# Giving the tiles of a decoder layer their own starting bytes in SBUF

## The chip, the core and the metric

The kernel runs on one core of a Trainium2 chip. The metric is the device time of one execution in microseconds; the runs of the kernel before took 2301.84 and 2302.49 us, median 2302.16 us. In the tables, PE is TensorE's matmul, PEld its weight load (the stationary operand), DVE, ACT and POOL are VectorE, ScalarE and GpSimd, and SP is the engine that issues nearly all transfers.

## The reference, cut to what matters

One decoder layer over 1024 positions of width 1024, in float32: a half feed-forward layer (SwiGLU, hidden width 2816), a mixer of two attentions with 8 heads of 64 each, a second half feed-forward layer, and a gated embedding.

```
x = x + 0.5 * swiglu(rms_norm(x, ffn1_norm), w_gate, w_up, w_down)
h = rms_norm(x, mix_norm)
fq, fk, fv, f_logit, sq, sk, sv, g_fox, g_sb = split_columns(h @ w_in)
y_fox = forgetting_attention(rms_norm(fq), rms_norm(fk), fv, log_f)
y_sb  = stick_breaking_attention(sq, sk, sv)
merged = sigmoid(g_fox) * (y_fox @ w_branch_fox) + sigmoid(g_sb) * (y_sb @ w_branch_sb)
x = x + merged @ w_out
x = x + 0.5 * swiglu(rms_norm(x, ffn2_norm), ...)
x = x + sigmoid(rms_norm(x, ple_norm) @ w_ple_gate) * (p @ w_ple_proj)
```

## The kernel before, in words

Each large product is written as float32 operands split in two: a rounded high part (fp32r) and the low remainder. A product is then three passes of matmuls, high by high, high by low, low by high, each with a stationary operand of 128 x 128 and a moving operand of up to 128 x 512. The two feed-forward layers and the output projection save matmuls by seven products of quarter blocks for eight, with sums of blocks formed beside.

The stages, by the profile's time: the start (0 to 41 us), the gate and up products of the first feed-forward layer (line 469, 41 to 473), its down product (line 364, 473 to 680), the projections of the mixer and the attention (lines 696, 704, 854, 935, 936, 987, 1009, 680 to 1417), the two branch products (line 1210, 1417 to 1478), the output projection (line 364), the second feed-forward layer (lines 424 and 469 to 1990, line 364 to 2197), and the gated embedding (line 1477, to the end). The order of the work on every engine is written out by hand.

Nearly all SBUF data passes through one pool, `sb`. The helper `slot(tag, shape)` takes the next buffer of a tag; the tags and their numbers of buffers stand in `BUFS`, and the buffers of a tag are used in turn. What the tags hold where the matmuls read them:

- line 469 (`product`): stationary is `hl`, a split weight block that rotates through the tags WL, WL, WL, Q, Q, PT; moving is one of seven blocks of activations `B[m]`: `B[1]`, `B[2]`, `B[5]`, `B[6]` in H, `B["12"]`, `B[7]` and `B[4]` in X, and `B[3]` in four T.
- line 364 (`matmuls` in `make_down`): both operands are in H, taken one after the other in `prep`, the activations (stationary) first and the weights (moving) second.
- lines 704 and 1210: stationary WH or WL (and others of a few), moving H. Lines 696 and 1477: stationary H, moving WH, WL, T, GF, RN, PT, Y. In the first eight units of line 696 the moving block has rows of 264 columns, 1056 bytes, so its four pieces begin 0, 32, 64 and 96 bytes further on modulo 256.
- line 1009: stationary X (the values), moving PT. Lines 935 and 936: stationary Q, moving KH and KL.

During a matmul PE also loads the stationary operand of the next one; the two operands of which this text speaks are those: the moving operand of one matmul, and the stationary operand that is loaded beside it. By "offset" is meant the first byte of the one less that of the other, modulo 256.

Where the buffers begin follows from the sizes and the order in which the pool meets the tags. In the kernel before, the first bytes modulo 256 are:

| tag | X | PT | H | T | WH | KH, KL | WL | Y | Q | GF, RN, RAW |
|---|---|---|---|---|---|---|---|---|---|---|
| buffers 1, 2, ... | 128, 128 | 128 x3 | 128 x4 | 128 x4 | 128, 0, 128 | 0, 0 | 0, 128, 0 | 128, 0 | 128, 128 | 128, 128 |

WH, WL and Y differ among themselves because their largest tile has 4224 bytes and not 4096.

Of the kernel before, what the change touches and what calls it, by code (L numbers as in the profile page):

```python
# [18 lines left out]
P = 128  # L19
# [10 lines left out]
PSUM = {"sc": 3, "pt": 2, "av": 1, "pf": 2}  # L30
BUFS = {"X": 2, "H": 4, "RAW": 2, "WH": 3, "WL": 3, "T": 4, "GF": 2, "RN": 2,
        "Q": 2, "KH": 2, "KL": 2, "Y": 2, "PT": 3}
FQ, FK, FV, FL, SQ, SK, SV, GFOX, GSB = 0, 512, 1024, 1536, 1544, 2056, 2568, 3080, 4104


@with_exitstack
def tile_hybrid_decoder_layer(
# [6 lines left out]
    nc = tc.nc  # L44
    cp = ctx.enter_context(tc.tile_pool(name="const", bufs=1))
    st = ctx.enter_context(tc.tile_pool(name="stats", bufs=4))
    sb = ctx.enter_context(tc.tile_pool(name="sb", bufs=2))
# [4 lines left out]
    def nm(s):  # L52
        uid[0] += 1
        return f"{s}_{uid[0]}"

    def slot(tag, shape, dt=F32):
        return sb.tile(shape, dt, tag=tag, bufs=BUFS[tag], name=nm(tag))

    def stat(shape, tag, bufs=4):
        return st.tile(shape, F32, tag=tag, bufs=bufs, name=nm(tag))  # L60
# [51 lines left out]
    def wraw_load(pieces, nk, n, tag="RAW"):  # L112
        raw = slot(tag, [P, nk, n])
        c = 0
        for src in pieces:
            w = src.shape[-1]
            nc.sync.dma_start(raw[:, :, c:c + w], src)
            c += w
        return raw
# [5 lines left out]
    def whigh(raw, nk, n, tag):  # L125
        hi = slot(tag, [P, nk, n], F32R)
        order("wh", nc.scalar.copy(hi[:], raw[:]))  # L127
        return hi

    def wlow(raw, hi, nk, n, tag, eng_lo=nc.gpsimd):  # L130
        lo = slot(tag, [P, nk, n], F32R)
        if nk == 1:
            parts = [(slice(None), slice(None), slice(i * n // 2, (i + 1) * n // 2)) for i in range(2)]
        else:
            parts = [(slice(None), slice(i * nk // 2, (i + 1) * nk // 2)) for i in range(2)]
        for part in parts:
            ins = eng_lo.tensor_sub(lo[part], raw[part], f(hi[part]))  # L137
            if eng_lo is nc.gpsimd:
                order("wl", ins)
        return lo  # L140
# [900 lines left out]
    def mix_start():  # L1041

        mx["v"], mx["qk"] = {}, {}
        mx["u1"] = v_units(FV + 256, NH, mx["v"])
        tags = (("T", "GF"), ("T", "Y"))
        mx["u2"] = fox_qk_units(FOX_PAIRS[0], mx["qk"], tags, "KH")
        q0 = FOX_PAIRS[0] * P
        pieces = [[kp(win)[:, 4 * kh:4 * kh + 4, a:a + n] for a, n in cols] for cols in (((FV + 256, 256 + NH),), ((FQ + q0, P), (FK + q0, P))) for kh in range(2)]
        raws = {}

        def load_v(X):
            raws["v"] = [wraw_load(pieces[kh], 4, 256 + NH, "Y") for kh in range(2)]

        def split_v(X):
            mx["v"]["w"] = [wsplit(raws["v"][kh], 4, 256 + NH, NAT[kh]) for kh in range(2)]

        def load_qk(X):
            raws["qk"] = [wraw_load(pieces[2 + kh], 4, 256) for kh in range(2)]

        def end(X, N):  # L1060
            hT.extend(halves(N))
            store_x(X, 1)
            for cell in loads[:2]:
                cell[1] = None
            side = posts(N[1], (24, 64, 104, 144), lambda: bank("pt"))
            side[48] = [lambda: mx["qk"].update(w=[wsplit(raws["qk"][kh], 4, 256, tags[kh]) for kh in range(2)])]
            weave(seq(*[g for _, g in mx["u1"][:4] + mx["u2"][:4]]), side)
        return {3: [load_v], 4: [split_v], 5: [lambda X: store_x(X, 0)], 6: [load_qk], "end": end}
# [164 lines left out]
    X = [slot("X", [P, 4, D]) for _ in range(2)]  # L1233
# [86 lines left out]
    X, N = ffn(N, ffn1_w_gate, ffn1_w_up, ffn1_w_down, mix_norm[0], x[0], ad[0], tags, first_entry, mix_start())  # L1320
# [178 lines left out]
    X, hT = [], []  # L1499
# [34 lines left out]
```

## Time and profile before

| | |
|---|---|
| median of two runs | 2302.16 us |
| profiled execution: span | 2300.6 us |
| instructions in it | 30661 |
| granted TensorE clock | 0.999 |
| PE busy, PEld busy | 2269.6, 1913.6 us |
| DVE, ACT, POOL busy | 1468.0, 980.7, 829.9 us |

The span runs from the first to the last instruction of the profiled execution; the runs' time holds some 1.6 us more. A row of the groups names the line, the engine, the operation, what is written and read (`ps<-H,WL`: the moving operand H, the stationary WL), the shape, the count, the busy time and the mean in ns of one. The duration of a matmul in these rows reaches from its start to the modelled end of its pipeline and so is longer than the distance to the next start: 12 matmuls with a mean of 389 ns begin 227 ns apart. A difference of durations between two groups of the same shape is nevertheless a difference of that distance, since the rest of it is the same.

### The profile page before, as it was taken

The page shows a single profiled execution, that of the slowest core. Times are in us where ns is not written, and L with a number is a line of the kernel's source. Part 1 is how long each engine was busy: PE and PEld are TensorE (multiplying, and loading weights), DVE is VectorE, ACT ScalarE, POOL GpSimd, SP SyncE. Part 2 cuts the span into 40 slices and gives each one's busy share as a digit, 9 for nine tenths or more (in the row PEclk, how much of TensorE's full clock was granted, in tenths as well). Part 3 has the DMA queues.
Part 4 walks back from the last instruction along what each step waited for, and adds up shares of the span by engine and source line. Part 5 has one row for each costly group of instructions (what it writes and reads, how often), then busy time and mean ns, then how long its engine had stood idle before and what let it go on. Part 6 is the DMA issues. An engine that isn't in the chain of part 4 may idle for free.

```text
span 2300.6 us, 30661 instructions
## 1 busy us (share of the span) xinstructions
PE 2269.6 (99%) x11466; PEld 1913.6 (83%) x11466; DVE 1468.0 (64%) x2199; ACT 980.7 (43%) x1742; POOL 829.9 (36%) x762
## 2 busy tenths in 40 slices
PE   9999999999999999899999999999999999999999
PEld 6888888888888999798988778888888888888887
DVE  8855555588863566456656766789645454778753
ACT  6433333333442555555555554246333333334431
POOL 2344444300033556545455645400534343200111
PEclk9999999999999999999999999999999999999999
DMA  3232323484332122422133235732423232655232
GB/s 138 92 124 83 124 83 123 142 307 168 103 120 75 52 79 74 137 79 71 50 82 89 74 115 199 258 139 74 138 78 128 78 128 78 226 213 205 70 106 92
DMA packets 188279, 275.49 MB, mean 120 GB/s; under 512 B 27097, under 2 KB 110297, under 8 KB 188130
## 3 DMA queue, kind: packets, MB, share of 16 engines
q1 hardware_dynamic: 188128, 273.53, 35.4%
q8 instruction: 90, 1.47, 0.3%
q14 instruction: 59, 0.48, 0.1%
q10 hardware_dynamic: 2, 0.00, 0.0%
HBM read 189.83 MB, written 75.27 MB: 115 GB/s over the span
## 4 chain that ended last, share of the span: by engine, by line
PE 55%; DVE 2%; ACT 1%; issue 0%; DVEq 0%; ACTq 0%
PE ps L469 18%; PE ps L364 12%; PE ps L704 9%; PE ps L1477 4%; PE ps L1210 4%; PE ps L1009 2%; PE ps L696 2%; PE ps L987 2%; DVE RN L911 1%; PE ps L424 1%; PE ps L936 1%; PE ps L935 1%; PE ps L854 1%; PE ps L224 0%; DVE H L104 0%
## 5 line engine op out<-in xcount | busy, mean ns | idle before, releaser
L364 PE MATMUL ps<-H,H 128*128 128x512 f32 x2184 | 497.8, 389 | 1.2 <-DVE X L372 1.2
L364 PEld LDWEIGHTS ps<-H,H 128*128 128x128 f32 x2184 | 409.3, 188 | 86.8 <-issue 2.0
L469 PE MATMUL ps<-H,WL 128*128 128x512 f32 x1008 | 244.6, 394 | 0.6 <-ACT WL L103 0.6
L469 PEld LDWEIGHTS ps<-H,WL 128*128 128x128 f32 x1008 | 189.7, 188 | 44.7 <-ACT WL L103 1.0
L704 PE MATMUL ps<-H,WH 128*128 128x512 f32 x768 | 209.5, 401 | 2.1 <-DVE PT L819 2.1
L137 POOL TENSOR_TENSOR WL<-RAW,WH 128x512 fp32r<-128x512 f32 (+1 forms) x108 | 129.4, 1219 | 101.2 <-ACT WH L127 72.9
L704 PEld LDWEIGHTS ps<-H,WH 128*128 128x128 f32 x768 | 136.8, 188 | 26.3 <-DVE PT L819 3.0
L990 DVE TENSOR_TENSOR PT<-ps,PT 128x512 fp32r<-128x512 f32 (+1 forms) x160 | 101.2, 633 | 84.4 <-ACT PT L989 83.6
L137 POOL TENSOR_TENSOR WL<-Y,WH 128x512 fp32r<-128x512 f32 (+1 forms) x10 | 14.4, 1465 | 383.1 <-ACT WH L127 383.1
L469 PE MATMUL ps<-H,Q 128*128 128x512 f32 x600 | 143.9, 390 | 0.0
L372 DVE SCALAR_TENSOR_TENSOR X<-ps,X 128x512 f32<-128x512 f32 x168 | 109.0, 685 | 50.9 <-PE ps L364 50.9
L696 PE MATMUL ps<-WH,H 128*128 128x256 f32 (+1 forms) x896 | 131.7, 286 | 2.0 <-ACT RN L753 0.7
L469 PEld LDWEIGHTS ps<-H,Q 128*128 128x128 f32 x600 | 112.6, 188 | 24.5
L989 ACT CAST PT<-ps 128x512 fp32r<-128x512 f32 (+1 forms) x160 | 87.2, 547 | 106.7 <-PE ps L987 102.1
L469 PE MATMUL ps<-X,WL 128*128 128x512 f32 x504 | 123.8, 394 | 0.0
L696 PEld LDWEIGHTS ps<-WH,H 128*128 128x128 f32 x896 | 116.5, 189 | 4.1 <-ACT RN L753 0.9
L469 PEld LDWEIGHTS ps<-X,WL 128*128 128x128 f32 x504 | 94.9, 188 | 22.0
L1009 PE MATMUL ps<-PT,X 128*128 128x256 f32 (+1 forms) x640 | 104.4, 283 | 8.8 <-DVE PT L990 8.8
L1009 PEld LDWEIGHTS ps<-PT,X 128*128 128x128 f32 x640 | 94.7, 190 | 21.0 <-DVE PT L990 11.0
L704 PE MATMUL ps<-H,WL 128*128 128x512 f32 x384 | 108.6, 404 | 0.0
L948 POOL TENSOR_TENSOR T<-T,l 128x128 f32<-128x128 f32 (+3 forms) x64 | 73.3, 1149 | 89.6 <-DVE l L947 87.2
L911 DVE TENSOR_TENSOR_SCAN RN<-GF,RN 128x127 f32<-128x127 f32 (+2 forms) x96 | 102.2, 1065 | 2.7
(400 smaller groups left out, 4680.0 us busy)
## 6 DMA issues: line engine op xcount, KB each, us to landing
hidden<-PT SPq DMA_DIRECT2D x40, 512.0 KB, 3.1
WH<-in_ffn_w_gate_dram SPq DMA_DIRECT2D x38, 512.0 KB, 5.0
Q<-hidden SPq DMA_DIRECT2D x24, 512.0 KB, 6.4
hidden<-RN SPq DMA_DIRECT2D x22, 512.0 KB, 2.6
RAW<-in_w_in_dram SPq DMA_DIRECT2D x22, 512.0 KB, 4.1
KH<-in_ffn_w_up_dram SPq DMA_DIRECT2D x20, 512.0 KB, 5.8
KL<-in_ffn_w_up_dram SPq DMA_DIRECT2D x20, 512.0 KB, 6.6
T<-in_ffn_w_down_dram SPq DMA_DIRECT2D x20, 512.0 KB, 4.4
```

What stands on the lines that cost most here:

```text
L137: ins = eng_lo.tensor_sub(lo[part], raw[part], f(hi[part]))
L364: pe(nc.tensor.matmul(groups[g][t][:], act[:, a, k, t * P:(t + 1) * P], wt[:, b, k, :], start=(fresh and n == 0), stop=(i in (6, 1, 4) and ...
L372: nc.vector.scalar_tensor_tensor(xs, groups[g][t][:], scale, xs, ALU.mult, ALU.add)
L469: pe(nc.tensor.matmul(ps[:], hl[:, a, k, :], rhs(m, b, k), start=(first and i == 0), stop=(final and i == 11), skip_group_check=True))
L696: pe(nc.tensor.matmul(ps[:, :n], hT[t // 4][a][:, k, (t % 4) * P:(t % 4 + 1) * P], w[k // 4][b][:, k % 4, :n], start=(i == 0), stop=(i == ...
L704: pe(nc.tensor.matmul(ps[:], w[a][:, k, :], hT[half][b][:, k, :], start=(i == 0), stop=(i == 23)))
L911: order("dve", nc.vector.tensor_tensor_scan(*args))
L989: high = nc.scalar.copy(pt[:, 0, :width], ps[:, :width])
L990: low = nc.vector.tensor_sub(pt[:, 1, :width], ps[:, :width], f(pt[:, 0, :width]))
L1009: pe(nc.tensor.matmul(o, lh, r, start=(kpair == c and i == 0), stop=(kpair == 0 and i == 3)))
L1210: pe(nc.tensor.matmul(ps[:], w[a][:, k, :], yT[g][b][:, k, half * 512:half * 512 + 512], start=(i == 0), stop=(i == 11)))
L1477: pe(nc.tensor.matmul(ps, hT[t // 4][a][:, k, (t % 4) * P:(t % 4 + 1) * P], pl["w"][d, k // 2][b][:, k % 2, cs], start=(i == 0), stop=(i = ...
```

## The change

Three things are changed, and all are about where in SBUF the tiles lie.

`slot` no longer takes a buffer of the size that is asked for, but one of a fixed size for each tag (`SIZE`, in elements of four bytes), and hands out a piece of it that begins `PLACE[tag]` elements into it. All the sizes are multiples of 256 bytes, so that all buffers begin at the same byte modulo 256, which is 128 in the built program. On that phase, the places put the tiles as follows (bytes beyond it, buffer by buffer):

| tag | X | H | WL | Q | PT | all others |
|---|---|---|---|---|---|---|
| bytes | 0, 96 | 0, 64, 0, 32 | 0, 64, 16 | 32, 96 | 0, 192, 8 | 0 |

The larger buffers need room, and the scratch that is kept for transfers whose descriptors are made on GpSimd is cut from 16384 to 8192 bytes a partition.

```
+SIZE = {"X": 4096 + 64, "H": 4096 + 64, "RAW": 1088, "WH": 1088, "WL": 1088 + 64, "T": 1024, "GF": 1024, "RN": 1024,
+        "Q": 1024 + 64, "KH": 1024, "KL": 1024, "Y": 1088, "PT": 1024 + 64}
+PLACE = {"X": (0, 24), "H": (0, 16, 0, 8), "WL": (0, 16, 4), "Q": (8, 24), "PT": (0, 48, 2)}
...
+    turns_of = {}
+
     def slot(tag, shape, dt=F32):
-        return sb.tile(shape, dt, tag=tag, bufs=BUFS[tag], name=nm(tag))
+        n = 1
+        for d in shape[1:]:
+            n *= d
+        i = turns_of.get(tag, 0)
+        turns_of[tag] = i + 1
+        o = PLACE.get(tag, (0,))
+        o = o[i % BUFS[tag] % len(o)]
+        t = sb.tile([P, SIZE[tag]], dt, tag=tag, bufs=BUFS[tag], name=nm(tag))[0:shape[0], o:o + n]
+        if len(shape) == 2:
+            return t
+        names = "abcd"[:len(shape) - 1]
+        return t.rearrange(f"p ({' '.join(names)}) -> p {' '.join(names)}", **dict(zip(names, shape[1:])))
...
-    nc = _bacc.Bacc("TRN2", target_bir_lowering=False, num_devices=1)
+    nc = _bacc.Bacc("TRN2", target_bir_lowering=False, num_devices=1, dynamic_dma_scratch_size=8192)
```

No instruction is added, removed or moved: on PE, DVE, ACT, POOL and SP the built program has the same instructions in the same order with the same waits, and only the addresses in them differ. Line numbers below line 32 rise by 3, those below `slot` by 16.

What the two address tables make of the pairs, counted over the built programs (matmuls, by the offset of the moving operand from the stationary one that is loaded beside it):

| line | before | after |
|---|---|---|
| 364 | 0: 2175 | 64: 1119, 32: 1056 |
| 469 | 0: 2352, 128: 1176 | 0: 664, 224: 490, 192: 385, 64: 349, 160: 348, 240: 346, 32: 297, ten more: 649 |
| 704 | 0: 654, 128: 432 | 0: 465, 64: 160, 32: 158, 192: 120, 240: 97, others 86 |
| 1210 | 0: 227, 128: 151 | 0: 258, others 120 |
| 1009 | 0: 576, 128: 15 | 160: 125, 192: 96, 0: 93, 168: 82, 8: 81, 96: 80, others 34 |

## The prediction

> **What bounds the kernel now.** I read the page first: its span, the share of each engine, and the chain that ended last.
>
> ```profile
> span 2300.6 us, 30661 instructions
> PE 2269.6 (99%) x11466; PEld 1913.6 (83%) x11466; DVE 1468.0 (64%) x2199; ACT 980.7 (43%) x1742; POOL 829.9 (36%) x762
> ```
>
> TensorE is busy in 99% of the span and every other engine has a third of it free. So only what changes the pace of matmuls counts, and the change touches nothing but addresses. The next view is therefore the chain that ended last, in order of time, with its longest pieces: there a piece of one line is an unbroken run of matmuls, and length over count is the distance between two starts.
>
> ```profile
> 1417.57 60.77 PE ps L1210 x264
> 1590.83 399.92 PE ps L469 x1740
> 1990.75 125.16 PE ps L364 x552
> ```
>
> All are 128x512 matmuls: line 364 steps by 125.16/552 = 226.7 ns, line 469 by 399.92/1740 = 229.8, line 1210 by 60.77/264 = 230.2. One shape, one engine, three paces. Why they differ is seen in the view of single lines (minimum, median and maximum duration of a group):
>
> ```profile
> L364 PE MATMUL ps<-H,H x2184: 387/389/477, 451.2 to 2202.5; 128*128 128x512 f32 x199
> L469 PE MATMUL ps<-H,WL x1008: 387/393/497, 56.7 to 1979.4; 128*128 128x512 f32 x168
> L469 PE MATMUL ps<-H,Q x600: 387/389/398, 78.9 to 1968.3; 128*128 128x512 f32 x150
> L469 PE MATMUL ps<-T,WL x240: 387/393/404, 70.6 to 1957.3; 128*128 128x512 f32 x120
> L469 PE MATMUL ps<-T,PT x96: 389/389/396, 164.4 to 1987.6; 128*128 128x512 f32 x96
> L704 PE MATMUL ps<-H,WH x768: 387/393/500, 719.8 to 1370.0; 128*128 128x512 f32 x192
> L704 PE MATMUL ps<-H,WL x384: 387/393/628, 723.5 to 1373.2; 128*128 128x512 f32 x192
> L1210 PE MATMUL ps<-H,WH x256: 387/392/477, 1373.4 to 1477.7; 128*128 128x512 f32 x128
> ```
>
> The tags sort them. Where all buffers of both tags begin at 128 modulo 256 (H, T, Q, PT) the median is 389; where one tag has buffers at 0 (WL: 0, 128, 0; WH: 128, 0, 128) it is 392 or 393. Line 469 shows both with the same moving block T: 393 beside WL, 389 beside PT. In order of time the same is seen as distances (start, length, line, names, count):
>
> ```profile
> 277.50 2.88 PE L469 MATMUL ps<-H,Q 128*128 128x512 f32 x12
> 280.22 2.89 PE L469 MATMUL ps<-T,PT 128*128 128x512 f32 x12
> 282.94 5.72 PE L469 MATMUL ps<-H,WL 128*128 128x512 f32 x24
> 288.50 2.96 PE L469 MATMUL ps<-X,WL 128*128 128x512 f32 x12
> 291.29 2.91 PE L469 MATMUL ps<-H,Q 128*128 128x512 f32 x12
> 294.04 2.88 PE L469 MATMUL ps<-X,Q 128*128 128x512 f32 x12
> 296.76 2.89 PE L469 MATMUL ps<-H,PT 128*128 128x512 f32 x12
> ```
>
> From start to next start: 226.7 ns a matmul for the first two rows (2.72/12), 231.7 for H,WL (5.56/24), 232.5 for X,WL, 229.2 for the first H,Q behind it, then 226.7 again. So offset 0 settles at 226.7 ns, offset 128 at about 232.5, and a run at 0 that follows one at 128 needs some matmuls to settle. What other offsets cost at 512 columns, no row shows.
>
> **The change, part by part.** *Instructions and waits.* None is added or moved; no wait is new, nothing is queued behind another thing. No row shows what addresses do to DVE, ACT and POOL; DVE is nearest to becoming the bound in the down product:
>
> ```profile
> 473.00:680.00 207.00, 205.42 (x974) 172.18 (x973) 165.70 (x200) 85.49 (x109) 20.71 (x27) 1.00 0.47 166
> L1009 PE MATMUL ps<-PT,X 128*128 128x256 f32 x512 | 102.8, 291 | 4.8 <-DVE PT L990 4.8
> q1 hardware_dynamic: 188128, 273.53, 35.4%
> ```
>
> There it is busy 165.7 of 207.0 us, so its operations would have to grow by a quarter before they set the pace; I cost that at nothing, between 0 and, if the third PT buffer (8 bytes off) slowed line 990 so that its wait of 4.8 us doubled, +5. The transfers take 35.4% of the sixteen DMA engines and their bytes stay the same: nothing. The scratch that is halved belongs to transfers issued by GpSimd, and the page's queues show none of data.
>
> *The pace of the matmuls* is what is left. The nearest row for offsets other than 0 and 128 is at the start of the mixer, where the moving block has rows of 1056 bytes, and its four pieces lie 0, 32, 64 and 96 bytes beyond the buffer's first byte modulo 256:
>
> ```profile
> 693.20 2.12 PE L696 MATMUL ps<-WH,H 128*128 128x264 f32 x16
> 695.15 1.15 PE L696 MATMUL ps<-WL,H 128*128 128x264 f32 x8
> ...
> 704.83 2.08 PE L696 MATMUL ps<-T,H 128*128 128x256 f32 x16
> ...
> 707.70 2.08 PE L696 MATMUL ps<-T,H 128*128 128x256 f32 x16
> ...
> 710.58 2.08 PE L696 MATMUL ps<-T,H 128*128 128x256 f32 x16
> ```
>
> Four units of 24 matmuls fill 693.20 to 704.83: 11.63/96 = 121.1 ns for 264 columns at mixed offsets. Two units fill 704.83 to 710.58: 5.75/48 = 119.8 for 256 columns at offset 0. The step from 256 to 512 columns at offset 0 is (226.7 - 119.8)/256 = 0.418 ns a column, so 264 columns at offset 0 would take 119.8 + 8 x 0.418 = 123.1. The mixed offsets are 2.0 ns a matmul cheaper. What does not grow with the columns is 226.7 - 512 x 0.418 = 12.7 ns at offset 0; that is the most that any placing can save.
>
> I take the 2.0 ns for every offset that is neither 0 nor 128, since it is the only row for such offsets, and so a pace of 224.7 ns at 512 columns. Offsets of 0 that remain (the table: 664 of 3528 on line 469) I don't count apart. The sum:
>
> - line 364, 2184 matmuls from 226.7 to 224.7: 4.4 us.
> - line 469, 3528 from 229.8 to 224.7: 18.0 us.
> - line 704, 1152: medians 4 ns above line 364's, so about 230.7, to 224.7: 6.9 us.
> - line 1210, 384 from 230.2 to 224.7: 2.1 us.
> - some 600 others of 512 columns (lines 424, 854, 935, 936, 1477), about 4 ns each: 2.4 us.
> - some 1,850 of 256 columns (lines 696 and 1009), 2.0 ns each: 3.7 us.
>
> That is 37.5 us. The attention's share of it (lines 704, 696, 1009: 10.6) lies beside waits for DVE and ACT, as the row of line 1009 shows with its 4.8 us; I let half of it, 5, go into those waits, which end no earlier. So 32 us: the profiled execution would come to 2268.6 us of span, and the median from 2302.2 to 2270.
>
> The bounds: if all 12.7 ns went, 512 columns would step by 214.0: 27.7 on line 364, 55.7 on 469, 19.2 on 704, 6.2 on 1210, 9 on the others, 23.5 on those of 256 columns, 141 us in all, 2161. If every pair came to the worst pace shown, 232.5: +12.7 on line 364, +9.5 on 469, some +4 on the rest, with the 5 of line 990 +31, 2333.
>
> *A rule to weigh.* The Trainium skill (TensorE: Matmul & The Clock Gate, "Back-to-back issue gap") gives the step from one isolated matmul to the next as N/2.4 + 2.5 ns, 216 ns at 512 columns; the trace's 226.7 is 11 above that, and by the rule as a floor all 7,850 matmuls of 512 columns would gain about 13 ns, 102 us, for some 2200. No run here shows that the distance to it is one of addresses.
>
> **The rivals.**
>
> *Offset 0 is the good one, and leaving it costs.* Line 364 now runs all its 2184 matmuls at the best pace that lasts, and Q and PT beside line 469 do too; the change takes offset 0 away from all of line 364. If 32 and 64 bytes behave at 512 columns as 128 does, it goes to 232.5: 2184 x 5.8 = +12.7 us, and line 469 to the same, 3528 x 2.7 = +9.5; with line 1009 and the rest +4 that is 2328, slower. For it speaks that the only offset shown at 512 columns costs 5.8; against it the 264-column rows. It decides when over half of the pairs that are neither 0 nor 128 step slower than 229.8.
>
> *Most of the fixed 12.7 ns is a clash of the two reads.* Then offsets can remove more than 2 ns: at half of it, 226.7 to 220.3 on line 364 and the others to the same, the lines give 14 + 33 + 12 + 4 + 5 + 12 = 80 us, less half of the attention's 24, so 68 and 2234; at all of it 2161. For it speaks that the minimum of 387 lies 2 below the settled 389, so that less is possible for single matmuls; against it that no run of matmuls holds such a pace.
>
> *Addresses do not matter, and the difference between the groups has another cause* (WL is written by other engines at other times than Q). Then nothing moves: 2302. Against it: T beside PT has 389 from its least to its median, T beside WL 393 in the same stage, though ScalarE and VectorE split both. This is what the Trainium skill says (same page, "Step-by-step: what each phase is for"): the two reads have ports of their own, and "Loading the next tile's weights doesn't steal SBUF read bandwidth from the running matmul". The 389 and 393 above, of one line and one moving tile, don't agree with it.
>
> **How the numbers follow.** The forecast, 2250 to 2297 with 2270 in it, has 0.54; more than 2 ns (2160 to 2250) 0.19; slower because offset 0 is lost (2305 to 2335, and beyond if an offset is worse than 128) 0.17; no effect (2297 to 2305) 0.10. The range leaves out the lower part of the second case and the upper of the third: 2205 to 2318. About 2% is what a measurement of this kernel can tell from no change: faster by that (under 2256) is the second case and a fifth of the first, 0.30; slower by that (over 2348) needs offsets worse than any shown, 0.04; within it 0.66.
>
> **What would show it.** In the profile after, the groups of line 380 (364 before) should have medians of about 387 for 389, those of line 485 (469) the same 387 for WL, Q and PT alike; the run of line 380 in the chain should step by 224.7. If line 380 shows 393 to 395, the first rival holds; 383 or less, the second. Unchanged medians by tag mean that addresses are not the cause. What would make the number wrong with the mechanism right is that 32 and 64 bytes differ from the mix in the 264-column rows, or that the sign of the offset counts: line 364 gets positive ones alone, line 469 both.

## The result, and the profile after

The changed kernel takes 2317.01 us (median of 2 runs, 2316.42 to 2317.60), against 2302.16: a ratio of 1.0065 with a 95% interval of 1.0046 to 1.0084. It is slower by 15 us; forecast were 2270 us. The range, 2205 to 2318, holds the time only because its upper end was drawn for a rival, so that is no success of the forecast. About 2% was named as what a measurement can tell from no change; these runs agree much better than that, and the sign is clear.

The page of the changed kernel opens as the page of before did:

```profile
span 2315.9 us, 30661 instructions
PE 2286.8 (99%) x11466; PEld 1913.3 (83%) x11466; DVE 1464.5 (63%) x2199; ACT 980.2 (42%) x1742; POOL 821.2 (35%) x762
```

The instructions are the same in number, the other engines are as busy as before or a little less, and PE alone is busy 17.2 us longer. The three long pieces of the chain that ended last (start, length, line, count) now are:

```profile
1423.59 61.12 PE ps L1226 x264
1598.77 402.87 PE ps L485 x1740
2001.64 127.48 PE ps L380 x552
```

Line 380 (364 before) steps by 127.48/552 = 230.9 ns where it stepped by 226.7, line 485 (469) by 231.5 where it was 229.8, line 1226 (1210) by 231.5 where it was 230.2. Times the number of matmuls that is 2184 x 4.2 = 9.2 us and 3528 x 1.7 = 6.1 us: 15.3, as much as the difference of the two spans, 2315.9 - 2300.6. That the two agree to a tenth is in part luck: the pace is that of one long piece, and smaller changes on other lines (the last 328 matmuls take 0.7 us more, line 712 0.7 less) cancel. TensorE's idle time did not grow: 31.0 us before, 29.1 now. Single lines (minimum, median, maximum):

```profile
L380 PE MATMUL ps<-H,H x2184: 387/394/482, 453.1 to 2217.1; 128*128 128x512 f32 x199
L485 PE MATMUL ps<-H,WL x1008: 387/394/499, 55.5 to 1990.1; 128*128 128x512 f32 x168
L485 PE MATMUL ps<-H,Q x600: 388/395/401, 77.9 to 1978.9; 128*128 128x512 f32 x150
L485 PE MATMUL ps<-T,WL x240: 387/394/398, 69.5 to 1967.7; 128*128 128x512 f32 x120
L485 PE MATMUL ps<-T,PT x96: 388/392/401, 164.2 to 1998.5; 128*128 128x512 f32 x96
L720 PE MATMUL ps<-H,WH x768: 387/394/504, 725.1 to 1375.9; 128*128 128x512 f32 x192
```

Before, two kinds of group could be told apart, 389 and 393. Now there is about one kind: the groups that had 389 (H,H; H,Q; T,PT) went to 392 to 395, and those that had 393 gained nothing. The same stretch of line 485 in order of time:

```profile
278.13 2.97 PE L485 MATMUL ps<-H,Q 128*128 128x512 f32 x12
280.94 2.92 PE L485 MATMUL ps<-T,PT 128*128 128x512 f32 x12
283.69 5.65 PE L485 MATMUL ps<-H,WL 128*128 128x512 f32 x24
289.18 2.95 PE L485 MATMUL ps<-X,WL 128*128 128x512 f32 x12
291.97 2.95 PE L485 MATMUL ps<-H,Q 128*128 128x512 f32 x12
294.75 2.96 PE L485 MATMUL ps<-X,Q 128*128 128x512 f32 x12
297.56 2.94 PE L485 MATMUL ps<-H,PT 128*128 128x512 f32 x12
```

From start to start H,Q steps by 2.81/12 = 234.2 ns and T,PT by 229.2, both 226.7 before; H,WL by 228.8 (231.7 before). Some pairs gain, more lose, and no row reaches 226.7.

### The profile page after: what moved, and what is told of

It is laid out like the page before. It is cut to its first block, busy times and chain, and to the rows that moved or that the text cites. A ratio compares the mean times of both kernels' runs of the same rounds, so it can differ in the third digit from the quotient of the medians.

```text
span 2315.9 us, 30661 instructions
## 1 busy us (share of the span) xinstructions
PE 2286.8 (99%) x11466; PEld 1913.3 (83%) x11466; DVE 1464.5 (63%) x2199; ACT 980.2 (42%) x1742; POOL 821.2 (35%) x762
## 4 chain that ended last, share of the span: by engine, by line
PE 55%; DVE 2%; ACT 1%; issue 0%; DVEq 0%; ACTq 0%
PE ps L485 18%; PE ps L380 12%; PE ps L720 8%; PE ps L1493 4%; PE ps L1226 4%; PE ps L1025 2%; PE ps L712 2%; PE ps L1003 2%; DVE RN L927 1%; PE ps L440 1%; PE ps L952 1%; PE ps L951 1%; PE ps L870 1%; PE ps L240 0%; DVE H L120 0%
## 5 line engine op out<-in xcount | busy, mean ns | idle before, releaser
L380 PE MATMUL ps<-H,H 128*128 128x512 f32 x2184 | 507.1, 393 | 0.8 <-DVE X L388 0.8
```

The lines of the kernel that those rows point to most:

```text
L380: pe(nc.tensor.matmul(groups[g][t][:], act[:, a, k, t * P:(t + 1) * P], wt[:, b, k, :], start=(fresh and n == 0), stop=(i in (6, 1, 4) and ...
```

## The experiments

Three theories were set against each other. Theory A: the offset between the two reads of a matmul (its moving operand, and the stationary one loaded beside it) sets the pace, and 0 is the best one. Theory B: something else in the change does it, the buffers' new sizes and order or the halved scratch. Theory C: the place of a tile by itself counts, not its distance from the other. All kernels are the changed kernel with another table of places, unless something else is said.

### All places at one phase

The places are taken out; sizes, buffers and scratch stay as changed, and all offsets between buffers are 0.

```diff
-PLACE = {"X": (0, 24), "H": (0, 16, 0, 8), "WL": (0, 16, 4), "Q": (8, 24), "PT": (0, 48, 2)}
+PLACE = {}
```

> The changed kernel with all places at 0: every tile begins at 128 modulo 256. Theory A (the pace of a matmul hangs on the offset between the moving operand and the stationary one that is loaded beside it, and 0 is the best): line 380 back at 226.7 ns, line 485 from 229.8 in the kernel before to about 227, and with line 720 and the rest some 15 to 20 us under the kernel before, 2282 to 2287. Theory B (the difference between the tags has another cause than the addresses, and the change lost its 15 us through the larger buffers or the halved scratch): 2317 as the changed kernel, medians 393 for WL and 389 for Q and PT.

Measured: 2291.29 us (5 runs, 2289.70 to 2291.70) beside 2301.52 for the kernel before on the same chip, a ratio of 0.9954 (0.9942 to 0.9966). That is faster, but less so than the 2282 to 2287 expected. Its chain, and rows of two of its lines:

```profile
1413.62 59.87 PE ps L1226 x264
1585.60 394.40 PE ps L485 x1740
1979.99 125.14 PE ps L380 x552
```

```profile
L485 PE MATMUL ps<-H,WL x1008: 387/389/497, 56.4 to 1968.7; 128*128 128x512 f32 x168
L485 PE MATMUL ps<-H,Q x600: 389/389/389, 78.3 to 1957.8; 128*128 128x512 f32 x150
L720 PE MATMUL ps<-H,WH x768: 387/393/504, 714.1 to 1366.1; 128*128 128x512 f32 x192
```

All three pieces step by 226.7 or 226.8 ns. WL, which had 393 in the kernel before, has 389 like Q: what set the two apart was the buffer's first byte and nothing about how or when it is written. The gain over before is nearly all line 485's, 3528 x (229.8 - 226.7) = 10.9 us; the long piece of line 1226 adds 0.9 (60.77 before, 59.87 now), and small changes elsewhere cancel. This version beats both kernels. What was missed is line 720: it keeps its 393 even with all its pairs at offset 0. The starts in the trace show where that comes from. Its matmuls stand in short stretches between those of other lines; the first seven distances of a stretch are 230.9 ns in the mean, and the few that come later (98 of 1040) 226.9. So in this version the excess over 226.7 on line 720 goes with the short stretches and not with the offset; what in an interruption costs it is not known.

### Only the scratch

The kernel before, with the smaller scratch and nothing else:

```diff
-    nc = _bacc.Bacc("TRN2", target_bir_lowering=False, num_devices=1)
+    nc = _bacc.Bacc("TRN2", target_bir_lowering=False, num_devices=1, dynamic_dma_scratch_size=8192)
```

> The kernel before with the scratch halved to 8192 bytes and nothing else: all tiles lie 8192 bytes lower and at the same byte modulo 256. Theory A: 2302, no difference. Theory B, in the form that the scratch cost the time: 2317.

Measured: 2302.17 us (10 runs), ratio 1.0002 (0.9993 to 1.0011). The scratch costs nothing. With the first experiment, where the new buffers and the scratch are all there and the kernel is faster, theory B is out.

### The places of H alone, and all others without H

```diff
+PLACE = {"H": (0, 16, 0, 8)}
```

> One phase, and H alone at 0, 64, 0, 32 bytes. Theory A: line 380 as in the changed kernel, 229 to 233 ns and 507 us busy; on line 485 two of seven moving blocks lie off, so a loss of 3 to 5 us there; in all 2296 to 2302. Theory B: 2317, as every kernel with the larger buffers.

```diff
+PLACE = {"X": (0, 24), "WL": (0, 16, 4), "Q": (8, 24), "PT": (0, 48, 2)}
```

> One phase, and X, WL, Q and PT at the places of the change, H at 0. Theory A: line 380 back at 226.7 ns (mean 389), 9 to 10 us under the changed kernel; line 485 still slow (medians 393 to 395); in all 2305 to 2309. Theory B: 2317.

Measured: 2308.53 us with H alone (7 runs, ratio 1.0029, 1.0019 to 1.0040) and 2308.28 with all but H (7 runs, 1.0029, 1.0018 to 1.0040). The chain with H alone:

```profile
1591.90 398.64 PE ps L485 x1740
1990.54 127.45 PE ps L380 x552
```

The chain with all but H:

```profile
1593.78 402.80 PE ps L485 x1740
1996.58 125.16 PE ps L380 x552
```

The two lines come apart as theory A says. H alone takes line 380 to 230.9 ns, the changed kernel's pace to the digit, and line 485 to 229.1. All but H leaves line 380 at 226.7 and takes line 485 to 231.5, again the changed kernel's pace. So the loss on line 380 comes from H's places and that on line 485 from the others. Against one phase (2291.29) they cost 17.2 and 17.0 us, and both together 25.7, not 34.2: line 485 is at 231.5 with H moved as well or without. An offset is a difference, so moving both operands isn't the sum of moving either.

H alone was slower than the 2296 to 2302 expected. There the loss on line 485 was put at 3 to 5 us and is 8.5, since the pairs that stay at offset 0 lose too: taking turns with moved ones they step by 228.0 ns in the mean (2518 of them), not by 226.7.

### One offset at a time

Every second buffer of H is moved by d bytes, so that all of line 380 has the one offset d (and so have 1008 of the 3528 matmuls of line 485, half of those that move H).

```diff
+PLACE = {"H": (0, d/4, 0, d/4)}
```

> One phase, and the second and fourth buffer of H 256 bytes further on: line 380 has all its 2184 matmuls at an offset of 256 bytes. Theory A with a period of 256: line 380 at 226.7 ns as at offset 0, the whole as with one phase, about 2291. Theory A without such a period (what counts is the distance in bytes): slower than 226.7, up to 233.

> One phase, and the second and fourth buffer of H 16 bytes further on. If the pace follows the distance from offset 0, it is just above 226.7 here, 227 to 229 (line 485 of the changed kernel has 229.2 at 16); if any offset but 0 breaks the settled state alike, 231 to 233.

> One phase, and the second and fourth buffer of H 32 bytes further on. If the pace is a matter of the pair alone, line 380 is at 233.2 ns throughout, 14 us above one phase; with the loss on line 485 the whole is 2308 to 2314.

> One phase, and the second and fourth buffer of H 64 bytes further on. In the changed kernel products at offset 64 and at 32 take turns on line 380, at 229.0 and 233.2 ns. If the pace is a matter of the pair alone, line 380 is at 229.0 here throughout (about 392 mean); if the turns with 32 spoiled 64, it is lower, down to 226.7.

> One phase, and the second and fourth buffer of H 128 bytes further on: line 380 has all its matmuls at offset 128. Theory A: 232 to 233 ns on line 380, as the pairs at 128 had on line 469 of the kernel before, so some 12 us more there and some 6 on line 485: 2305 to 2312.

> One phase, and the second and fourth buffer of H 192 bytes further on, an offset of minus 64. If the sign has no meaning, 229 ns on line 380 as at 64; if it counts, as line 485 of the changed kernel suggests, 232 to 233.

> One phase, and the second and fourth buffer of H 224 bytes further on, an offset of minus 32. Theory A with the sign without meaning: line 380 at 233 ns as at plus 32 in the changed kernel, the whole 2305 to 2312. With a sign that counts: another pace, 227 to 231.

Of each chain the piece of line 380, in the order 256, 16, 32, 64, 128, 192, 224:

```profile
1976.13 125.13 PE ps L380 x552
```

```profile
1991.40 127.89 PE ps L380 x552
```

```profile
1995.71 128.82 PE ps L380 x552
```

```profile
1989.08 126.38 PE ps L380 x552
```

```profile
1995.01 128.81 PE ps L380 x552
```

```profile
1993.62 128.81 PE ps L380 x552
```

```profile
1995.96 128.81 PE ps L380 x552
```

Divided by 552, and with the times (one run each but for offset 0, beside 2300.76 to 2301.73 for the kernel before):

| offset, bytes | 0 (one phase) | 256 | 16 | 32 | 64 | 128 | 192 | 224 |
|---|---|---|---|---|---|---|---|---|
| pace, ns | 226.7 | 226.7 | 231.7 | 233.4 | 228.9 | 233.3 | 233.3 | 233.3 |
| time, us | 2291.29 | 2287.20 | 2306.85 | 2313.29 | 2303.14 | 2312.33 | 2310.88 | 2313.46 |

The pace repeats after 256 bytes, 0 is the best of the seven places, and 64 is the least bad of the others. 192 is 64 in the other direction and costs 6.6 ns where 64 costs 2.2, so the sign counts there; 32 and 224 cost the same. At 16 the expectations left 227 to 229 open, for a pace that grows with the distance from 0; 231.7 speaks against that. The changed kernel can be put together from the table: half of its line 380 at 64 and half at 32 gives (228.9 + 233.4)/2 = 231.15, 4.4 above 226.7, times 2184 = 9.7 us, and 9.2 were found.

The time at 256 lies 4 us below that of one phase, with equal paces; the profiled executions differ by 3.8 us in span. That is the granted clock of these executions and not the offset. At the start, line 216's second eight matmuls step by 427 ns in the trace of one phase and by 216 in that of 256, which is then 1.9 us ahead where line 380 begins. Later one phase has a granted clock of 0.50 from 944.9 to 948.3 us and again about 1358 to 1361 us, where 256 has 1.00, and each costs it another 0.9 us. From line 1226 on nothing is added. So the single times in the table can hold up to 4 us that are not of the offset; the paces don't.

On line 380 the stationary operand loaded beside a matmul and the matmul's own lie at the same byte modulo 256 nearly throughout, so these runs don't tell which of the two counts.

### All tiles moved alike

One phase again, with a tile of 64 bytes ahead of the pool, so that every tile lies 64 bytes further on and no offset between two of them changes (line numbers rise by 1).

```diff
+    cp.tile([P, 16], F32, name="space")
```

> One phase, and all buffers of the pool 64 bytes further on together (a small tile that nothing uses lies ahead of them), so that every pair is at offset 0 and every tile at 192 modulo 256. Theory A (only the offset between the two counts): 226.7 ns on line 380 and 2291 as with one phase. Theory C (each tile's own place counts, and 128 is a good one): slower, 2300 or more.

Measured: 2291.78 us, against 2291.29 at one phase and 2303.14 where half of H alone moved by the same 64 bytes. Its chain:

```profile
1586.25 394.40 PE ps L486 x1740
1980.65 125.13 PE ps L381 x552
```

Both pieces are those of one phase. At this one shift, where a tile lies by itself doesn't count for the pace; theory C, by which it was to take 2300 us or more, is out, and theory A stands.

### 256 columns in place of 512

What was left is why the 264-column rows of the prediction pointed the other way. In the runs above the 256-column matmuls of line 712 gave a hint: between their starts were 119.2 ns at offset 0 (mean of some 1200), but 116.7 at 192 and 116.4 at 64 (394 each; the stationary operand is H there, so that H moved by 64 gives 192). Either the number of columns turns the order round (theory D), or line 712's short units, with other work between them, tell nothing of the offset (theory E). So the long runs of line 381 got 256 columns, with every second buffer of H moved by 0, 64 and 128 bytes (line numbers rise by 1 in them):

```diff
-                n = 0
-                for a, b in ((0, 0), (0, 1), (1, 0)):
-                    for k in range(nk):
-                        pe(nc.tensor.matmul(groups[g][t][:], act[:, a, k, t * P:(t + 1) * P], wt[:, b, k, :], start=(fresh and n == 0), stop=(i in (6, 1, 4) and n == 3 * nk - 1), skip_group_check=True))
-                        n += 1
+                for h in (0, 256):
+                    n = 0
+                    for a, b in ((0, 0), (0, 1), (1, 0)):
+                        for k in range(nk):
+                            pe(nc.tensor.matmul(groups[g][t][:, h:h + 256], act[:, a, k, t * P:(t + 1) * P], wt[:, b, k, h:h + 256], start=(fresh and n == 0), stop=(i in (6, 1, 4) and n == 3 * nk - 1), skip_group_check=True))
+                            n += 1
```

The work on TensorE is that of the whole product in twice as many matmuls. These versions serve the measurement alone: the down products come out changed.

> All places 0, and the down products and the output projection take their matmuls in two halves of 256 columns (4368 for 2184 on that line). Theory D (the number of columns decides which offset is good): the long runs of that line step by 119.2 ns, as the 256-column matmuls of line 712 do at offset 0 in the other runs. Theory E (offset 0 is best at any width, and line 712's units are too short to show it): it steps by half of 226.7, 113.4, or by a little more. Under both the time is about 2291 + 4368 x 119.2 ns - 2184 x 226.7 ns = 2317 (D), or about 2292 (E).

> The same with every second H buffer 64 bytes on, so that the 256-column matmuls of that line have offset 64. Theory D: they step by 116.5 ns, as line 712's did at 64 and 192, and so 2.7 faster than at offset 0 (11.8 us over 4368), where at 512 columns offset 64 was 2.2 slower. Line 485 and the others lose the 11 us that they lost in h64, so the whole time stays about that of w256_o0. Theory E: they step 1.1 ns (half of 2.2) or more slower than at offset 0, and the time is some 16 us above w256_o0.

> The same with every second H buffer 128 bytes on. Theory D: 118.5 ns, 0.7 faster than at offset 0, as line 712 showed at 128. Theory E: 3.3 ns (half of 6.6) or more slower than at offset 0; by it the time is 14 us and more above w256_o64's, by theory D about 9.

The line's group and a long piece of the chain, offset 0:

```profile
L381 PE MATMUL ps<-H,H 128*128 128x256 f32 x4368 | 526.5, 283 | 0.3
```

```profile
1995.17 141.11 PE ps L381 x1176
```

Offset 64:

```profile
L381 PE MATMUL ps<-H,H 128*128 128x256 f32 x4368 | 516.9, 279 | 0.6 <-DVE X L389 0.6
```

```profile
1998.36 130.04 PE ps L381 x1104
```

Offset 128:

```profile
L381 PE MATMUL ps<-H,H 128*128 128x256 f32 x4368 | 524.8, 283 | 0.2
```

```profile
2003.05 141.12 PE ps L381 x1176
```

At 256 columns offset 0 steps by 141.11/1176 = 120.0 ns and offset 64 by 130.04/1104 = 117.8. Offset 128 shows 120.0 in this piece and 119.6 in the mean over its 4349 distances without a wait. The order is turned round: 64 is 2.2 ns better than 0 here and 2.2 worse at 512 columns, and the whole times agree (2317.82, 2318.17, 2326.38: offset 64 wins 9.6 us on this line and loses about as much on the 512-column lines that share H). Theory D holds at 64, with 2.2 for the 2.7 that it expected. At 128 it expected 0.7 below offset 0 and 0 to 0.4 are found; theory E's 3.3 above is further off. Offset 64 is the one place at which the sign is shown to turn in long runs, with one run for each offset. What makes 256 and 512 columns differ is not settled.

## Why the prediction was wrong, step by step

*What bounds the kernel* held: PE at 99%, no more idle time than before, and the change is found in the distances between matmuls. That the distance in long runs goes by the offset modulo 256, and not by tag, writer or scratch, held too. It was argued there from groups; one phase, the scratch alone and the shift of all tiles show it.

*The step that failed* is "I take the 2.0 ns for every offset that is neither 0 nor 128, since it is the only row for such offsets". It had three faults. It carried a price from 264 columns to 512, and the sign can turn between widths: at 64 bytes -2.2 at 256 columns, +2.2 at 512 (264 columns themselves were not run at one offset). And it took one price for all offsets: at 512 columns they cost from +2.2 (64) to +6.7 (32), and none is below offset 0. And the row was not quite what it was taken for: its moving pieces lie in two buffers that begin 128 bytes apart, so that they run through all eight multiples of 32, 0 and 128 among them, and the 123.1 for offset 0 beside them was worked out from other widths and not measured. In place of 224.7 line 380 came to 230.9. So the term of line 364, -4.4 us, became +9.2, and that of line 469, -18.0, became +6.1.

*The attention's terms* (lines 704, 696, 1009: 10.6 us, half of it counted) came to nothing: from the starts, +0.2, -0.7 and +0.2 us, without what they wait for. Line 696 got cheaper offsets at 256 columns and gained its 0.7. Line 704 was at 231 ns and stayed there; its term, 6.9 us, took the whole excess over 224.7 for a matter of offset, and the version at one phase shows 230.5 with every pair at 0, in its short stretches. (The "some 600 others" are 744 by their groups, which moves the sum by 0.6 us.) The down product's DVE and the third PT buffer cost nothing, as taken:

```profile
L1025 PE MATMUL ps<-PT,X 128*128 128x256 f32 x512 | 103.1, 291 | 4.8 <-DVE PT L1006 4.8
```

The wait for VectorE is the 4.8 us of before; the bound of +5 wasn't needed.

*The rivals.* The first, that offset 0 is the good one, is what happened, with its place right and its price too high: it put all offsets at 128's 232.5, and 64 bytes, over half of line 364, cost 2.2 and not 5.8 (9.2 us for its 12.7; 6.1 for its 9.5 on line 469; nothing for its +4 on the rest). Its point of decision, over half of the moved pairs slower than 229.8, was passed: of some 6,050 distances at 512 columns with offsets other than 0 and 128, about 4,850 are at offsets whose mean on their line is above that. For it spoke the only offset that had been measured at 512 columns in the very lines at stake; that row should have outweighed a finer extrapolation from another width. The second, that most of the fixed 12.7 ns is a clash that offsets can remove, has no support at 512 columns: 226.7 is the lowest settled pace of all places tried. The Trainium skill's isolated gap (TensorE: Matmul & The Clock Gate, "Back-to-back issue gap") is 216 ns at 512 columns; the split float32 matmuls came to it in no run by any placing. The bfloat16 matmuls at the start do: in the trace with H at 256 bytes, line 216's second eight, at offset 0 with a reload each, step by 226 ns once and then by 216. So at offset 0 there still are some 11 ns that these places didn't remove; whether they go with the data type is not tested. The third rival, that addresses don't matter, is out. The Trainium skill's sentence (same page, "Step-by-step: what each phase is for") that loading the next weights takes nothing from the running matmul does not agree with this kernel: one and the same 2184 matmuls step by 226.7 or 233.4 ns according to where the two reads lie to each other. By what way the one read slows the other no run shows.

*What would make the number wrong* named both things that did: 32 and 64 bytes differ from the mix of the 264-column rows, and the sign counts (192 costs three times what 64 does). It named them as what could change the number; they changed the direction.

## What to carry to other kernels

Where long runs of matmuls with a reload each bound a kernel, look at the first byte of the moving operand and of the stationary operand loaded beside it, modulo 256, since 1 to 3% of the pace hang on it: of the places tried here the same byte is best for 512 columns, and 64 bytes apart for 256. A pool whose tags have tiles of different sizes spoils this unseen; buffers of sizes that are multiples of 256 bytes, all at one phase, gained half a per cent here. Where the matmuls of a line stand in short stretches between others, as on line 720, placing the tiles gained next to nothing. And a price read at one shape is not carried to another, not even its sign: where one row at the right shape stands against a finer working from the wrong one, the first sets the forecast and the second the range.

## What the runs showed of the hardware

- The settled pace of a 128x512 fp32r matmul with a reload goes by the offset of the two reads modulo 256 bytes, and a shift of all tiles by 64 bytes leaves it as it is: 226.7 ns at 0 and 256, 228.9 at 64, 231.7 at 16, 233.3 to 233.4 at 32, 128, 192 and 224.
- At 128x256 the order is another: 120.0 at 0, 119.6 to 120.0 at 128, 117.8 at 64.
- The two settled paces at offset 0 differ by 226.7 - 120.0 = 106.7 ns for 256 columns, 0.417 ns a column. A line through the two leaves 13.3 ns that don't grow with the columns (226.7 - 213.4).
- Distances need time to settle: in the prediction's rows a run of 12 at offset 0 behind one at 128 still had 229.2. In the changed kernel, where offsets change every 12 or 24 matmuls, offset 0 on line 485 came to 228.9 in the mean. With every pair of the line at offset 0, line 720's short stretches still begin at 230.9 and come to 226.9 from the eighth distance on.
- Executions differ in when the full clock is granted: in five of the 17 traces the second eight bfloat16 matmuls at the start step by 216 ns, in the others by 427, which was worth 1.9 us between the two compared above.
